# U blocks split in two turns, retrieval head by head, head innermost, and closer gather rows: one transformer layer with a product-key expert layer

## The chip, the cores and the metric

The kernel runs on 1 core of a Trainium2 chip. The metric is the device time of one launch in microseconds; the median of three runs counts. Engines: PE (matmuls), DVE (vector), ACT (scalar, activations), POOL (here the indirect DMAs), SP (the DMA queue for loads and stores).

## What is computed

One layer over 512 tokens of width 1024 in f32: three mixers side by side (stick-breaking attention, a gated recurrence, attention into 256 memory tokens), an output projection, and an expert layer whose experts are single neurons. The last one fills most of the time. Cut to its core:

```
h = rms_norm(x + mixed @ w_out)
q = (h @ w_query).reshape(t, 8 heads, 2, 128)
scores = einsum('thcd,hcnd->thcn', q, sub_keys)          # 128 keys per half
top_s, top_i = top_k(scores, 16)                         # per head and half
cand_s = top_s[..0, :, None] + top_s[..1, None, :]       # 16 x 16 sums
cand_i = top_i[..0, :, None] * 128 + top_i[..1, None, :]
best_s, pos = top_k(cand_s, 16)
gate = softmax(best_s);  expert_idx = take(cand_i, pos)
act = gelu(einsum('td,thkd->thk', h, expert_u[expert_idx]))
out = x + einsum('thk,thkd->td', gate * act, expert_v[expert_idx])
```

There are 128 x 128 = 16384 experts, so `expert_u` and `expert_v` have 16384 rows of 1024 each.

## The kernel before

The work is written as some twenty Python generators ("threads") that a class `Threads` runs by a planner, `Pace`: it keeps a clock for each engine, prices every operation from two cost tables, and lets the thread that is due next record its operations up to its next `yield`. What is recorded is the order of each engine's queue; engines then run in that order and wait for each other by semaphores. A `yield "name"` waits for a flag that another thread sets by `th.set("name")`; a `yield` of a number puts the thread off by that many planned nanoseconds. All engine calls go through one helper (line 203), so the rows below name tiles.

A matmul in f32 quality is made of three (`mm3`): a factor is split into a rounded part (`hi`, written by ACT) and the rest (`lo`, by DVE), and hi·hi, lo·hi and hi·lo are summed. `whi`/`wlo` are those parts of weights, `h2hi`/`h2lo` of the normed tokens, `xhi`/`xlo` of expert rows.

The 512 tokens are four tiles of 128. Up to some 350 us the mixers run. From there the expert layer begins, first for tile 0 (`GT`), then for tiles 1 to 3 (`DENSE`): `outproj` (PE, `op`; DVE adds it into `xr`), `norm2` (ACT `sq`, DVE's short `rv`, `rq`, `rs`, PE transposes `xt`, DVE `mxT`, ACT and DVE `h2hi` and `h2lo`), `query` (PE `qp` or `qf` for q, `qs` for the scores, which ACT copies to `sc` or `sct`), and `topk` on DVE. `query` goes by heads, with a `w` of each head split into `whi` and `wlo`; its matmuls fill up with other work, for GT with the mixers' last transposes.

`topk` takes one tile after another. For each pair of a head's two halves `top16` does MAX, FIND and REPLACE on both, and after a `yield` MAX and FIND again; 8 such units per tile, then 4 on 50 candidates each. Then comes a chain over 128 x 2048 f16 elements (`ge`, `gw`, with the helper tile `tkb`), in which one-hot comparisons and products and `fold` give both key numbers of each pick; `IJ` holds these and the gate. For GT `eidx` holds the row numbers of its experts.

GT's experts are then gathered: `gather` fetches one row per token by an indirect DMA on POOL, four ahead, and DVE multiplies and sums it (`row`, 128 times from `expert_u`, then `xg`, 128 times from `expert_v`). `pace_rows` spaces rows by `GAPS`: 1900 ns until the dense query is done, then 8000 ns until all gates are ready, and from there by the blocks that are left.

The other three tiles go through all 16384 experts: 128 U blocks of 128 experts (`dense`: a block is loaded as `ex` by SP, split into `xhi` and `xlo` in pages of a pool of eight, multiplied in 24 matmuls into `ua`, and ACT writes the gelu `gel`, which is stored), and 128 V blocks (`gel` times gates `G` gives `w`, its parts `whi` and `wlo`, summed in `pin`). Between them stand the gates: `gprep` transposes `IJ` (PE `gt`) and makes `gpg`, `gbuild` one-hots on DVE (`oh`), `grest` finishes them on ACT, `gsum` multiplies them on PE (`gb`), ACT copies to `stg` and stores to `gd` in HBM, from where `G` is loaded. This runs beside the U blocks; when the last gate's flag is set, `dense` puts up to `TRANS` = 9 more U blocks in its order and goes over to V. The flags of the query that `topk` waits for are `q{t}`, one for each tile, set when all heads are done.

Of the kernel before, what the change touches and what calls it, by code (L numbers as in the profile page):

```python
# [8 lines left out]
F32R = mybir.dt.float32r  # L9
# [11 lines left out]
P = 128  # L21
D = 1024
# [18 lines left out]
UA = 3  # L41


GAPS = (1900.0, 8000.0)
BLOCK = 4150.0, 0.95
GP = 8000.0
ND2 = 500.0
# [216 lines left out]
def tile_trunk_layer(ctx: ExitStack, tc: tile.TileContext, x, mem, w_in, w_kv, w_out, w_query,  # L264
# [748 lines left out]
    def query(ts):  # L1013
        yield f"h2{ts[0]}"
        if not kst:
            kst["k"] = [page([P, 8, NKEY], name="keys") for _ in range(2)]
            for i in range(2):
                SP.dma_start(kst["k"][i], keys_t[:, 8 * i:8 * i + 8])
        keys = kst["k"]
        for t in ts:  # L1020
            if t in DENSE[1:]:
                b3 = big3([P, 3, 1024], name="sct")
                sc[t] = [b3[:, i].rearrange("p (g n) -> p g n", g=8) for i in range(2)]
                tka[t] = b3[:, 2]
            else:
                sc[t] = [page([P, 8, P], name="sc") for _ in range(2)]
        pend = []

        def tail():
            t, h, q = pend.pop(0)  # L1030
            b = bank("qx")
            for c in range(2):
                PE.transpose(b[:, c * P:(c + 1) * P], q[:, c * P:(c + 1) * P], ident)
            qT = t2([P, 256], name="qT")
            A.activation(qT, b[:, :256], AF.Copy)
            pend2.append((t, h, qT))

        def tail2():
            t, h, qT = pend2.pop(0)
            b = bank("qs")  # L1040
            for c in range(2):
                PE.matmul(b[:, c * P:(c + 1) * P], qT[:, c * P:(c + 1) * P], keys[h // 4][:, 2 * (h % 4) + c], start=True, stop=True)
            A.activation(sc[t][h // 4][:, 2 * (h % 4):2 * (h % 4) + 2], b[:, :256].rearrange("p (c n) -> p c n", c=2),
                         AF.Copy)

        def tailf():
            qT = [pendf.pop(0), pendf.pop(0)]
            h = donef.pop(0)
            bs = [bank("qs") for _ in range(2)]
            o = [bs[i // 2][:, (i % 2) * 256:(i % 2) * 256 + 256] for i in range(ND)]  # L1050
            for i in range(ND):
                for c in range(2):
                    PE.matmul(o[i][:, c * P:(c + 1) * P], qT[c][:, i * P:(i + 1) * P], keys[h // 4][:, 2 * (h % 4) + c],
                              start=True, stop=True)
            for i, t in enumerate(ts):
                A.activation(sc[t][h // 4][:, 2 * (h % 4):2 * (h % 4) + 2], o[i].rearrange("p (c n) -> p c n", c=2), AF.Copy)

        pend2, pendf, donef = [], [], list(range(QF, PH))
        for h in range(PH):
            W = ws.get()  # L1060
            if h == PH - 1 and ts is DENSE:
                th.set("q_last")
            if ts is DENSE and h >= QF:
                for c in range(2):
                    b = bank("qf")
                    for k in range(KD):
                        w, lw = [x[k // 4][:, k % 4, c * P:(c + 1) * P] for x in W]
                        mm3(b[:, :TD], w, lw, hsl(h2hi, k, 0, TD), hsl(h2lo, k, 0, TD), k == 0, k == KD - 1)
                    qT = t2([P, TD], name="qT")
                    A.activation(qT, b[:, :TD], AF.Copy)  # L1070
                    if pend2:
                        tail2()
                    if pend:
                        tail()
                    elif len(pendf) > 1:
                        tailf()
                    pendf.append(qT)
                    yield
                continue
            for t in ts:  # L1080
                if th.later(f"h2{t}"):
                    yield f"h2{t}"
                b = bank("qp")
                if t == GT:
                    proj_t(W, 0, b[:, :256], *[[h] for h in gat["hT"]])
                else:
                    proj_t(W, DENSE.index(t), b[:, :256], h2hi, h2lo)
                q = t2([P, 256], name="q")
                A.activation(q, b[:, :256], AF.Copy)
                if pend2:  # L1090
                    tail2()
                if pend:
                    tail()
                pend.append((t, h, q))
                yield
        if ts is DENSE:
            th.set("q_mm")
        while pend or pend2 or pendf:
            if pendf:
                tailf()  # L1100
            if pend2:
                tail2()
            if pend:
                tail()
            yield
        for t in ts:
            th.set(f"q{t}")
# [1 line left out]
    tk = {}  # L1109

    def topk(t):
        yield f"q{t}"
        c_start, c_len, c_rank = [c[:, :, None, :].to_broadcast([P, 16, 32, 4]) for c in tkc]
        pa = tka[t] if t in tka else page([P, 1024], name="tka")
        pb = page([P, 1024], name="tkb")
# [2 lines left out]
        def top16(srcs, vs, ix):  # L1118

            for k in (0, 8):  # L1120
                for s, v in zip(srcs, vs):
                    V.max(v[:, k:k + 8], s)
                for s, v, i in zip(srcs, vs, ix):
                    V.max_index(i[:, k:k + 8], v[:, k:k + 8], s)
                if k == 0:
                    for s, v in zip(srcs, vs):
                        V.match_replace(s, v[:, 0:8], s, FILL)
                yield "v"

        for g in range(0, 16, 2):  # L1130
            gs_ = (g, g + 1)
            yield from top16([sc[t][i // 8][:, i % 8] for i in gs_], [vals[:, i] for i in gs_], [idx[:, i] for i in gs_])
        idf = pa[:, 512:768].rearrange("p (h c k) -> p h c k", c=2, k=16)
        V.tensor_copy(idf.rearrange("p h c k -> p (h c) k"), idx)
# [24 lines left out]
            yield from top16([cand[:, i] for i in hs_], [best[:, i] for i in hs_], [pos[:, i] for i in hs_])  # L1159

        IJ = sb.tile([P, 3, 128], F32, name=f"IJ{t}", tag="ij", bufs=2)
        gate = IJ[:, 2].rearrange("p (h k) -> p h k", h=8)
        V.tensor_tensor(gate, best, best[:, :, 0:1].to_broadcast([P, 8, 16]), op=OP.subtract)
        A.activation(gate, gate, AF.Exp)

        posb = pb[:, 400:464].bitcast(F16)
        V.tensor_copy(posb, pos.rearrange("p h k -> p (h k)"))
        ge = page([P, 16, 128], F16, name="ge")
        g4 = ge.rearrange("p r (a b) -> p r a b", b=4)
        V.tensor_tensor(g4, posb.rearrange("p (a b) -> p a b", b=4)[:, None].to_broadcast([P, 16, 32, 4]), c_start,  # L1170
# [3 lines left out]
        def fold(w, dst):  # L1174
# [11 lines left out]
        i1 = pb[:, 528:592].bitcast(F16).rearrange("p (r h) -> p r h", h=8)  # L1186
        V.tensor_copy(i1, idf[:, :, 1, :].rearrange("p h r -> p r h"))
        w = page([P, 16, 128], F16, name="gw")
        V.tensor_tensor(w.rearrange("p r (h k) -> p r h k", h=8), ge.rearrange("p r (h k) -> p r h k", h=8),
                        dI[:, :, :, None].to_broadcast([P, 16, 8, 16]), op=OP.mult)  # L1190
        yield "v"
        yield from fold(w, IJ[:, 0])
        yield "v"
# [6 lines left out]
        V.tensor_tensor(g4, bb.rearrange("p (a b) -> p a b", b=4)[:, None].to_broadcast([P, 16, 32, 4]), c_rank,  # L1200
                        op=OP.is_equal)
        yield "v"
        V.tensor_tensor(ge.rearrange("p r (h k) -> p r h k", h=8), ge.rearrange("p r (h k) -> p r h k", h=8),
                        i1[:, :, :, None].to_broadcast([P, 16, 8, 16]), op=OP.mult)
        yield "v"
        yield from fold(ge, IJ[:, 1])
        yield "v"
# [108 lines left out]
    def dense():  # L1316
# [6 lines left out]
                store[b] = raw([P, D], name="ex")  # L1323
                SP.dma_start(store[b], src[b])

        def split(rw, dst, b, eng, pg):
            if b >= NBLK or b in dst:
                return
            hi = pg([P, D], F32R, name="xhi")
            A.activation(hi, rw[b], AF.Copy)  # L1330
            lo = pg([P, D], F32R, name="xlo")
            eng.tensor_tensor(lo, rw[b], f(hi), op=OP.subtract)
            dst[b] = (hi, lo)

        def u_prep(b):
            for i in range(b, b + 3):
                load(ur, u_t, i)
            split(ur, us, b, V, wpage)

        def u_mm(b):  # L1340
            blocks[0] -= 1
# [86 lines left out]
        pace.late = True  # L1428
        u_prep(0)
        u_prep(1)  # L1430
        yield "q_mm"
        while vi < NBLK:
            ready = all(f"G{t}" in th.flags for t in DENSE)
            if ui < NBLK and (not ready or ui < vi + LA):
                u_prep(ui + 2)
                u_mm(ui)
                ui += 1
                yield "pe"
# [7 lines left out]
            if not pins:  # L1446
                for i in range(3, 3 + UA):
                    load(ur, u_t, ui + i)
                g_load(0)
                while uo and uo[0][0] < 4:  # L1450
                    u_gelu()
                gel_back(0)
                for i in range(min(TRANS, NBLK - ui)):
                    u_prep(ui + 2)
                    u_mm(ui)
                    ui += 1
                    if i == VT:
                        gel_back(1)
                        vhi(0)
                    yield "pe"  # L1460
                gel_back(1)
                vhi(0)
                prep1(0)
                prep2(0)
                prep1(1)
                vhi(1)
                for _ in range(2 * ND):
                    pins.append(bank("pin"))
# [138 lines left out]
```

## Time and profile before

| | |
|---|---|
| median of 3 runs | 1612.44 us (1610.82 to 1612.53) |
| profiled execution | 1616.55 us, of which the span of the instructions is 1614.5 us |
| mean granted clock of PE | 0.988 of full |
| PE busy | 1567.7 us, 97% of the span |
| DVE, ACT, POOL busy | 78%, 49%, 21% |
| chain that ended last | PE 95%, DVE 2%, ACT 1%, DMA 1% |
| DMA | 424 MB, 263 GB/s on average |

An engine's busy share tells little by itself: the stages have different limits. The chain is followed back from the last instruction, at each step to what released it. In timelines, the bracket behind a row is the time that the engine stood idle before it and the instruction that ended this.

### The profile page before, as it was taken

Reading aid. Unit: us, or ns where it says so; the run is one execution under the profiler, and the core shown is the slowest. Engines: PE = TensorE matmul, PEld = TensorE weight load, DVE = VectorE, ACT = ScalarE, POOL = GpSimd, SP = SyncE. Lnnn points to the kernel's source line nnn. Section 1 sums busy time; section 2 is a strip of 40 time slices with the busy share of each in tenths; the row PEclk is TensorE's granted clock in tenths of the full one; section 3 lists DMA queues with packets and bytes.
Section 4 is the critical chain, followed back from the end, with each engine's and each line's share of the span. In section 5 each row is a group of like instructions: output and inputs, shape, how many; then the busy total and the mean of one; then the engine's idle time right before and its main releaser. Section 6 shows DMA issues by size and latency. Waiting matters only on the chain.

```text
span 1614.5 us, 25732 instructions
## 1 busy us (share of the span) xinstructions
PE 1567.7 (97%) x9359; PEld 1436.4 (89%) x9359; DVE 1260.6 (78%) x2499; ACT 790.6 (49%) x1559; POOL 337.8 (21%) x340
## 2 busy tenths in 40 slices
PE   6999999998999999999999999969999999999998
PEld 5998998898999999999999999968888888888886
DVE  5466568779768798778887966739888988998997
ACT  5422258764434336677566777733333333333332
POOL 3000000000251111112011111233343434343430
PEclk9999999999999999999999999979999999999999
DMA  6232102264497767888788889899999999999993
GB/s 248 81 103 79 53 27 91 81 229 163 155 358 251 233 217 246 268 259 282 256 277 264 267 282 292 277 313 407 408 408 399 393 393 380 395 387 396 380 384 121
DMA packets 164239, 424.03 MB, mean 263 GB/s; under 512 B 13584, under 2 KB 62736, under 8 KB 164112
## 3 DMA queue, kind: packets, MB, share of 16 engines
q1 hardware_dynamic: 68256, 238.21, 41.0%
q0 software_dynamic: 36864, 134.23, 22.7%
q10 hardware_dynamic: 58992, 49.95, 9.3%
q8 instruction: 73, 1.20, 0.3%
q14 instruction: 54, 0.44, 0.1%
HBM read 368.20 MB, written 54.13 MB: 262 GB/s over the span
## 4 chain that ended last, share of the span: by engine, by line
PE 95%; DVE 2%; ACT 1%; DMA 1%; issue 0%; DVEq 0%; SPq 0%; ACTq 0%
PE ua L203 33%; PE pin L203 32%; PE pf L203 5%; PE pt L203 4%; PE qf L203 4%; PE sz L203 3%; PE gb L203 3%; PE op L203 3%; PE qp L203 2%; PE hs L203 2%; PE so L203 1%; PE qs L203 1%; DMA gd<-stg 1%; ACT se L203 0%; PE mo L203 0%; PE nt L203 0%
## 5 line engine op out<-in xcount | busy, mean ns | idle before, releaser
L203 DVE TENSOR_TENSOR xlo<-ex,xhi 128x1024 fp32r<-128x1024 f32 x256 | 312.5, 1221 | 118.6 <-ACT xhi L203 109.2
L203 POOL DMA_INDIRECT row<-in_u_rows_dram,eidx x128 | 156.1, 1219 | 977.0 <-ACT whi L203 402.2
L203 PE MATMUL ua<-h2hi,xhi 128*128 128x384 f32 x1024 | 348.6, 340 | 0.0
L203 PE MATMUL ua<-h2hi,xlo 128*128 128x384 f32 x1024 | 342.8, 335 | 0.0
L203 PE MATMUL ua<-h2lo,xhi 128*128 128x384 f32 x1024 | 342.5, 335 | 0.0
L203 ACT ACTIVATE whi<-w 128x384 fp32r<-128x384 f32 (+1 forms) x205 | 144.9, 724 | 345.1 <-DVE w L203 325.8
L203 PE MATMUL pin<-xhi,whi 128*128 128x512 f32 x768 | 300.1, 391 | 12.1 <-ACT whi L203 12.1
L203 PE MATMUL pin<-xlo,whi 128*128 128x512 f32 x768 | 299.9, 391 | 0.9 <-DVE xlo L203 0.9
L203 PE MATMUL pin<-xhi,wlo 128*128 128x512 f32 x768 | 299.7, 390 | 0.0
L203 ACT ACTIVATE xhi<-ex 128x1024 fp32r<-128x1024 f32 x256 | 268.3, 1049 | 28.6 <-DMA ex<-in_v_rows_dram 14.2
L203 DVE TENSOR_TENSOR wlo<-w,whi 128x384 fp32r<-128x384 f32 (+1 forms) x204 | 161.0, 804 | 99.7 <-ACT whi L203 51.2
L203 POOL DMA_INDIRECT row<-in_v_rows_dram,eidx x128 | 164.7, 1286 | 251.2 <-DVE xg L203 175.8
L203 PEld LDWEIGHTS ua<-h2lo,xhi 128*128 128x128 f32 x1024 | 192.5, 188 | 0.0
L203 PEld LDWEIGHTS ua<-h2hi,xhi 128*128 128x128 f32 x1024 | 192.2, 188 | 0.0
L203 PEld LDWEIGHTS ua<-h2hi,xlo 128*128 128x128 f32 x1024 | 192.2, 188 | 0.0
L203 PEld LDWEIGHTS pin<-xhi,whi 128*128 128x128 f32 x768 | 144.8, 189 | 42.5 <-ACT whi L203 12.4
L203 PEld LDWEIGHTS pin<-xlo,whi 128*128 128x128 f32 x768 | 144.8, 189 | 31.5 <-DVE xlo L203 1.4
L203 PEld LDWEIGHTS pin<-xhi,wlo 128*128 128x128 f32 x768 | 144.7, 188 | 30.3
L203 DVE SCALAR_TENSOR_TENSOR xg<-row,wgt,xg 128x1024 f32<-128x1024 f32 x128 | 163.9, 1280 | 1.0
L203 DVE CUSTOM_DVE_ANT_0 row<-row,xr 128x1024 f32<-128x1024 f32 x128 | 154.6, 1218 | 6.8 <-issue 6.6
L203 ACT ACTIVATE oh<-oh,gpg 128x128 f16<-128x128 f16 x384 | 126.5, 436 | 26.7 <-DVE oh L203 6.8
L203 ACT ACTIVATE gel<-ua 128x384 f32<-128x384 f32 x128 | 62.7, 490 | 156.4 <-PE ua L203 151.0
(255 smaller groups left out, 2299.5 us busy)
## 6 DMA issues: line engine op xcount, KB each, us to landing
ex<-in_u_t_dram SPq DMA_DIRECT2D x128, 512.0 KB
ex<-in_v_rows_dram SPq DMA_DIRECT2D x128, 512.0 KB
gd<-stg ACTq DMA_DIRECT2D x48, 512.0 KB
G<-gd SPq DMA_DIRECT2D x48, 512.0 KB
gel<-gel ACTq DMA_DIRECT2D x63, 384.0 KB
gel<-gel SPq DMA_DIRECT2D x63, 384.0 KB
w<-in_w_query_dram SPq DMA_DIRECT2D x32, 512.0 KB
w<-in_w_in_dram SPq DMA_DIRECT2D x26, 512.0 KB
```

The source lines that it names most:

```text
L203: r = fn(*args, **kw)
```

## The change

Four things. (1) The U blocks: `u_prep` now loads and rounds a block (`xhi`, on ACT) three blocks ahead of its matmuls, and a new `u_rest` takes the rest (`xlo`, on DVE) two blocks ahead, where both stood at two blocks; loads are made as far ahead as before. (2) `query` sets a flag `s{t}_{h}` behind each head's score copy, and `topk` waits for the flag of each unit's head in place of `q{t}`. (3) The gate, the positions and the two products hold the 128 picks of a token as [k, h], the head innermost, where they stood as [h, k]; so the factor that is the same for all k of a head is no longer repeated along the innermost axis. (4) `GAPS` for the rows after the query falls from 8000 to 6000 ns.

```diff
-GAPS = (1900.0, 8000.0)
+GAPS = (1900.0, 6000.0)
...
             A.activation(sc[t][h // 4][:, 2 * (h % 4):2 * (h % 4) + 2], b[:, :256].rearrange("p (c n) -> p c n", c=2),
                          AF.Copy)
+            th.set(f"s{t}_{h}")
...
                 A.activation(sc[t][h // 4][:, 2 * (h % 4):2 * (h % 4) + 2], o[i].rearrange("p (c n) -> p c n", c=2), AF.Copy)
+                th.set(f"s{t}_{h}")
...
     def topk(t):
-        yield f"q{t}"
+        yield f"s{t}_0"
...
             gs_ = (g, g + 1)
+            yield f"s{t}_{g // 2}"
...
-        gate = IJ[:, 2].rearrange("p (h k) -> p h k", h=8)
+        gate = IJ[:, 2].rearrange("p (k h) -> p h k", h=8)
...
-        V.tensor_copy(posb, pos.rearrange("p h k -> p (h k)"))
+        V.tensor_copy(posb.rearrange("p (k h) -> p h k", h=8), pos)
...
-        V.tensor_tensor(w.rearrange("p r (h k) -> p r h k", h=8), ge.rearrange("p r (h k) -> p r h k", h=8),
-                        dI[:, :, :, None].to_broadcast([P, 16, 8, 16]), op=OP.mult)
+        V.tensor_tensor(w.rearrange("p r (k h) -> p r k h", h=8), ge.rearrange("p r (k h) -> p r k h", h=8),
+                        dI[:, :, None, :].to_broadcast([P, 16, 16, 8]), op=OP.mult)
...
-        V.tensor_tensor(ge.rearrange("p r (h k) -> p r h k", h=8), ge.rearrange("p r (h k) -> p r h k", h=8),
-                        i1[:, :, :, None].to_broadcast([P, 16, 8, 16]), op=OP.mult)
+        V.tensor_tensor(ge.rearrange("p r (k h) -> p r k h", h=8), ge.rearrange("p r (k h) -> p r k h", h=8),
+                        i1[:, :, None, :].to_broadcast([P, 16, 16, 8]), op=OP.mult)
...
         def u_prep(b):
-            for i in range(b, b + 3):
+            for i in range(b, b + 2):
                 load(ur, u_t, i)
-            split(ur, us, b, V, wpage)
+            if b < NBLK:
+                us[b] = [wpage([P, D], F32R, name="xhi")]
+                A.activation(us[b][0], ur[b], AF.Copy)
+
+        def u_rest(b):
+            if b < NBLK:
+                lo = wpage([P, D], F32R, name="xlo")
+                V.tensor_tensor(lo, ur[b], f(us[b][0]), op=OP.subtract)
+                us[b].append(lo)
...
             if ui < NBLK and (not ready or ui < vi + LA):
-                u_prep(ui + 2)
+                u_prep(ui + 3)
+                u_rest(ui + 2)
                 u_mm(ui)
```

How the rows of an engine's queue stand at three places, first DVE in the query of GT, from the mixers' sum `oss` on. The `wlo` are parts of query weights, one pair for each head. Before:

```order
L203 TENSOR_REDUCE oss_3466<-o_3415 128x12
L203 TENSOR_SCALAR rv_3469<-oss_3466 128x12
L203 TENSOR_TENSOR wlo_3473<-w_3321,whi_3471 128x1024
L203 TENSOR_TENSOR wlo_3477<-w_3323,whi_3475 128x1024
L203 TENSOR_TENSOR rq_3522<-rr_3519 128x12
```

The same place after:

```order
L203 TENSOR_REDUCE oss_3474<-o_3423 128x12
L203 TENSOR_SCALAR rv_3477<-oss_3474 128x12
L203 MAX tka_3415<-sc_3205 128x8 x2
L203 MAX_INDEX tka_3415<-tka_3415,sc_3205 128x8 x2
L203 TENSOR_TENSOR wlo_3485<-w_3321,whi_3483 128x1024
L203 TENSOR_TENSOR wlo_3489<-w_3323,whi_3487 128x1024
L203 MAX tka_3415<-sc_3205 128x8 x2
L203 MAX_INDEX tka_3415<-tka_3415,sc_3205 128x8 x2
L203 MATCH_REPLACE sc_3205<-tka_3415,sc_3205 128x128 x2
L203 TENSOR_TENSOR rq_3540<-rr_3531 128x12
```

A second half of a top-k unit (MAX and MAX_INDEX, which the profile calls MAX8 and FIND_INDEX8) now stands ahead of this pair, and a first half behind it; seven rows further on, in both orders, the `wlo` of head 7 follow.

DVE again, where the first rows of the gather arrive, during head 3 and 4 of the dense query; `eidx` holds the row numbers, `row` with `act` is one gathered row (an ISA pair). Before:

```order
L203 SCALAR_TENSOR_TENSOR eidx_4565<-IJ_4342 128x128
L203 TENSOR_TENSOR wlo_4569<-w_4236,whi_4567 128x1024
L203 TENSOR_TENSOR wlo_4573<-w_4238,whi_4571 128x1024
L203 ISA row_4619,act_4617<-row_4619,xr_2623 128x1024
L203 ISA act_4617 128x1
```

The same place after, from the first row on:

```order
L203 ISA row_4550,act_4548<-row_4550,xr_2623 128x1024
L203 ISA act_4548 128x1
L203 MAX tka_4540<-sc_4268 128x8 x2
L203 MAX_INDEX tka_4540<-tka_4540,sc_4268 128x8 x2
L203 ISA row_4552,act_4548<-row_4552,xr_2623 128x1024
L203 ISA act_4548 128x1
L203 MAX tka_4540<-sc_4268 128x8 x2
L203 MAX_INDEX tka_4540<-tka_4540,sc_4268 128x8 x2
L203 MATCH_REPLACE sc_4268<-tka_4540,sc_4268 128x128 x2
L203 ISA row_4554,act_4548<-row_4554,xr_2623 128x1024
L203 ISA act_4548 128x1
L203 TENSOR_TENSOR wlo_4606<-w_4280,whi_4604 128x1024
```

Before, the pair of `wlo` behind `eidx` is head 4's; after, head 3's stands there, and head 4's (here `wlo_4606`) has moved behind the first three rows.

Last, DVE in the U blocks where the third dense tile's one-hots begin (`gpg` is made from the transposed `IJ`, `oh` are the one-hots). Before:

```order
L203 TENSOR_SCALAR gpg_10372<-gt_10285 128x128
L203 CAST gpg_10372<-gt_10285 128x2x64x2
L203 CAST gpg_10372<-gpg_10372 128x128
L203 TENSOR_TENSOR gpg_10372<-gpg_10372 128x128
L203 ISA row_10007,act_4617<-row_10007,xr_2623 128x1024
L203 ISA act_4617 128x1
L203 TENSOR_TENSOR oh_10380<-io2_6103,gpg_10372 128x1024
L203 TENSOR_TENSOR oh_10380<-oh_10380,gpg_10372 128x512
L203 TENSOR_TENSOR oh_10383<-io2_6103,gpg_10372 128x1024
```

The same place after:

```order
L203 TENSOR_SCALAR gpg_10428<-gt_10354 128x128
L203 CAST gpg_10428<-gt_10354 128x2x64x2
L203 CAST gpg_10428<-gpg_10428 128x128
L203 TENSOR_TENSOR gpg_10428<-gpg_10428 128x128
L203 TENSOR_TENSOR oh_10433<-io2_5831,gpg_10428 128x1024
L203 TENSOR_TENSOR oh_10433<-oh_10433,gpg_10428 128x512
L203 TENSOR_TENSOR oh_10436<-io2_5831,gpg_10428 128x1024
L203 TENSOR_TENSOR oh_10436<-oh_10436,gpg_10428 128x512
L203 TENSOR_TENSOR oh_10452<-io2_5831,gpg_10428 128x1024
```

The row of the gather that stood between `gpg` and the first one-hot is gone from there. On PE, between this tile's `gt` and its second to fourth `gb` stand three U blocks, where four stood.

## Rows read from the trace of the kernel before

**Rows 1.** PE's waits, whole run: waited for, us in total, times, longest us

```profile
PE pin L203 <- ACT whi L203: 12.1, 1, 12.1
...
PE qf L203 <- issue: 2.5, 3, 1.2
```

**Rows 2.** Busy us (x instructions) by stretch: PE, PEld, DVE, ACT, POOL; clock, DMA, GB/s

```profile
700.00:800.00 100.00, 100.00 (x664) 97.76 (x663) 86.99 (x211) 66.30 (x153) 14.87 (x13) 1.00 0.83 274
...
1200.00:1300.00 100.00, 100.00 (x443) 82.80 (x442) 89.59 (x105) 35.77 (x50) 38.36 (x30) 1.00 1.01 398
```

**Rows 3.** Timeline of DVE in GT's query: start, us, operation [idle before]

```profile
340.38 2.36 DVE L203 TENSOR_TENSOR wlo<-w,whi 128x1024 fp32r<-128x1024 f32 x2 [1.89 <-ACT whi L203]
...
360.28 0.48 DVE L203 MAX8 tka<-sc 128x8 f32<-128x128 f32 x2
...
361.71 0.68 DVE L203 TENSOR_TENSOR mxl<-mxT,mxh 128x512 fp32r<-128x512 f32 x1
362.31 0.48 DVE L203 MAX8 tka<-sc 128x8 f32<-128x128 f32 x2
...
363.23 0.47 DVE L203 MAX8 tka<-sc 128x8 f32<-128x128 f32 x2
```

**Rows 4.** Timeline of PE, single rows from 349 to 941 us

```profile
349.70 0.39 PE L203 MATMUL qp<-wlo,h2g 128*128 128x256 f32 x1 [0.27 <-DVE wlo L203]
...
399.74 1.97 PE L203 MATMUL xt<-ident,sq 128*128 128x128 f32 x8 [3.68 <-ACT sq L203]
...
441.09 0.33 PE L203 MATMUL qf<-h2hi,wlo 128*128 128x384 f32 x1
441.26 0.33 PE L203 MATMUL qf<-h2hi,whi 128*128 128x384 f32 x1
...
449.51 0.34 PE L203 MATMUL qf<-h2hi,wlo 128*128 128x384 f32 x1 [1.20 <-issue]
...
940.66 0.49 PE L203 MATMUL gt<-ident,IJ 128*128 128x128 f32 x3
```

**Rows 5.** Timeline of DVE at the first rows of the gather

```profile
431.79 0.28 DVE L203 SCALAR_TENSOR_TENSOR eidx<-IJ 128x128 int32<-128x128 f32 x1
...
441.82 1.23 DVE L203 CUSTOM_DVE_ANT_0 row<-row,xr 128x1024 f32<-128x1024 f32 x1 [6.64 <-issue]
```

**Rows 6.** DVE's groups by shape, 391 to 960 us: busy us, mean ns

```profile
L203 DVE TENSOR_TENSOR gw<-ge,tkb 128x2048 f16<-128x2048 f16 x4 | 9.1, 2284 | 0.0
...
L203 DVE TENSOR_TENSOR ge<-ge,c 128x2048 f16<-128x2048 f16 x4 | 4.9, 1219 | 0.0
```

**Rows 7.** Timeline of DVE and ACT at the third dense tile's first one-hots

```profile
944.63 1.23 DVE L203 TENSOR_TENSOR xlo<-ex,xhi 128x1024 fp32r<-128x1024 f32 x1 [3.53 <-ACT xhi L203]
...
947.91 0.69 DVE L203 TENSOR_TENSOR oh<-io,gpg 128x1024 f16<-128x1024 f16 x1
...
948.63 1.32 ACT L203 ACTIVATE oh<-oh,gpg 128x128 f16<-128x128 f16 x4 [2.29 <-DVE oh L203]
948.98 0.69 DVE L203 TENSOR_TENSOR oh<-io,gpg 128x1024 f16<-128x1024 f16 x1
```

**Rows 8.** Timeline of ACT, SP and DVE from the last U to the first V block

```profile
1062.59 1.33 ACTq L203 DMA_DIRECT2D gd<-stg  x2
...
1072.77 0.32 SPq L203 DMA_DIRECT2D G<-gd  x1
...
1077.70 0.56 DVE L203 TENSOR_TENSOR w<-gel,G 128x384 f32<-128x384 f32 x1 [17.58 <-issue]
...
1080.58 1.06 ACT L203 ACTIVATE xhi<-ex 128x1024 fp32r<-128x1024 f32 x1 [14.21 <-DMA ex<-in_v_rows_dram]
```

**Rows 9.** Stretches around the first V block, columns as in rows 2

```profile
1067.00:1072.00 5.00, 3.00 (x18) 2.68 (x16) 0.00 (x0) 0.00 (x0) 0.94 (x1) 1.00 1.06 358
...
1082.00:1089.00 7.00, 5.96 (x13) 4.40 (x14) 5.94 (x9) 2.99 (x5) 1.05 (x2) 0.50 1.03 416
```

**Rows 10.** Timeline of DVE at the end

```profile
1609.26 1.28 DVE L203 SCALAR_TENSOR_TENSOR xg<-row,wgt,xg 128x1024 f32<-128x1024 f32 x1
```

More of the change, by code (lines that the diff above doesn't have):

```diff
@@ L1324, in load @@
                 SP.dma_start(store[b], src[b])
[L1326 to L1333, printed above, removed]
         def u_prep(b):
-            for i in range(b, b + 3):
+            for i in range(b, b + 2):
                 load(ur, u_t, i)
-            split(ur, us, b, V, wpage)
+            if b < NBLK:
[6 more added lines that the diff above has]
+                us[b].append(lo)
         def u_mm(b):
@@ L1430, in dense @@
         u_prep(1)
+        u_rest(0)
+        u_prep(2)
+        u_rest(1)
         yield "q_mm"
@@ L1453, in dense @@
                 for i in range(min(TRANS, NBLK - ui)):
-                    u_prep(ui + 2)
+                    u_prep(ui + 3)
+                    u_rest(ui + 2)
                     u_mm(ui)
```

## The prediction

> **What bounds the kernel now.** I read the share of busy time first, then PE's waits, then the table of stretches, and only then timelines at the places where PE waits. The table [rows 2] shows a PE that is busy for 100 of 100 us in the middle of the U blocks and again in the V blocks, at the full granted clock, while DVE is at 87 to 90. In those stretches nothing that DVE, ACT or a queue gains can shorten the run, unless it removes a wait somewhere else. What can move is the list of PE's waits [rows 1]: 12.1 us before the first V block and 2.5 of `issue` in the query; then 3.68 before the last of three `xt` transposes and 0.27 for a `wlo` [rows 4], and the waits of the first 300 us, which the change does not touch. A price per microsecond follows: where PE is the bound, a microsecond of wait is a microsecond of the run. A longer wait costs more, since after one the clock is at half for a while: from 1082 to 1089 us PE works at a granted clock of 0.50 of full, that is at 1.2 of 2.4 GHz [rows 9], right after it stood idle for some 12 us; 7 us at half speed lose 3.5 us.
>
> **The head-innermost layout.** It changes no count. Per token tile `gw` (2284 ns, x4) and the second product on `ge`, which is of the same form, have a factor repeated along the innermost axis; after the change that axis holds 8 neighbouring heads. The nearest row is an operation of the same 2048 elements and the same type without such a repeat, `ge<-ge,c` at 1219 ns [rows 6]. I take that one: 8 x (2284 - 1219) = 8.5 us of DVE. The dearer end is no gain at all; the conversion of `posb` and the subtraction for `gate` now write with a stride, on 128 elements each, which I take as nothing, covered by PE at 100 of 100 us. All four tiles' products lie beside PE's matmuls, so by itself this is worth 0; it counts through DVE's queue below.
>
> **Top-k by head, GT's query.** A top-k unit now waits for one head's scores and not for all eight, so units enter DVE's queue among the `wlo` of the same query. A unit's first half (two MAX, two FIND, two REPLACE) takes 361.71 - 360.28 = 1.43 us, its second 363.23 - 362.31 = 0.92 us [rows 3]. The first half lands ahead of the `wlo` at 340.38, which today follows 1.89 us of idle: covered, cost 0. The next second half (0.92) and first half (1.43) land ahead of the `wlo` of head 7, with no idle time to hide them. Today PE already waits 0.27 us for that `wlo` at 349.70 [rows 4], so there is no slack: 0.92 + 1.43 = 2.35, less a little that the earlier `wlo` gains: **+2.2 us** (0.5 if DVE's small operations there shrink, 3.9 if the wait halves the clock for 3.5 us).
>
> **Norm of the dense tiles.** PE waits 3.68 us at 399.74 and less at two more `xt` [rows 4]; each waits for ACT's `sq`, which waits for four short DVE operations that stand behind top-k pieces. These units are earlier now, so at this point DVE is already in the 50-wide folds of the candidates, and two tiles' short operations stand back to back. Adding up DVE's rows between the same marks in both orders, the first tile comes later and the last about 0.9 us earlier: **-0.9 us** (-2 to +1).
>
> **First rows of the gather.** `eidx` is done at 431.79 and the first row reaches DVE at 441.82, 10.0 us later, of which DVE stood idle 6.64 [rows 5]. Today head 4's `wlo` stands ahead of that wait; now it stands behind it and behind three rows. What is queued behind the waiting row operation is thus a `wlo` that PE wants: PE reads the first `wlo` of head 4 at 441.09 [rows 4], about 442.4 with the +2.2 and -0.9 above. DVE has some 5 us less to do before `eidx` (2.1 from GT's two products, some 3 of units that slipped into idle time), so I put `eidx` at 426 and the first row at 436.0. Then three rows (1.3 us each with the read of the sum), two second halves or so of units between them (0.92 and 1.43), and one `wlo` of 1.2: 436.0 + 3.9 + 2.35 + 1.2 = 443.4 against 442.4. **+1.0 us** (0 if `eidx` is at 425, +4 if at 429).
>
> **The `issue` wait.** At 449.51 PE waits 1.20 us for nothing that the profile shows [rows 4], the first of three such waits of 2.5 us together [rows 1], with a lower clock after them; in all about 3.4 us. It falls into the stretch in which the first ten rows are fetched. The change leaves ten rows there, a few us earlier: **0** (-3.4 if it vanishes, +2 if it lasts longer). The Trainium skill (Runtime: NRT & Kernel Launch, Instruction fetch mechanics) says that instructions are refilled by DMA in blocks of 256 and that this is hidden by the pace of issue. By that these waits could not be a fetch; the trace has an idle PE with no semaphore behind it while the DMA engines are full, which speaks against the word hidden, and no run here shows yet which it is. By the rule the wait would follow some other cause, and the term stays 0 either way.
>
> **U two and three blocks ahead.** ACT's `xhi` moves one block earlier, DVE's `xlo` stays. Today DVE waits for `xhi`, 3.53 us of it at 944.63 [rows 7], and PE does not wait for DVE there: 100 of 100 us [rows 2]. The hi and lo pages alternate over eight buffers, so now `xlo` reuses the page of the block three before, and DVE may wait for PE's end of that block in place of `xhi`. A block is 24 matmuls 0.17 us apart [rows 4], some 4.15 us, and `xlo` has over one block of slack left: **0**. One place is tight: for the third dense tile the order puts its second to fourth `gb` behind three U blocks after `gt` where four stood. Today DVE needs 3.3 us from 944.63 to the first `oh` (`xlo`, four small operations, a row of 1.14) and 1.07 for each pair of `oh` [rows 7]. After, that is 2.1 without the row, 3.2 for three pairs, 3.4 for another `xlo`, a row and the fourth pair, and 1.3 on ACT: 10.0 us, to 954.6 if DVE starts as late as today. The last of these `gb` is due at 940.66 + 0.6 for `gt` and a `gb` [rows 4] + 3 x 4.15 = 953.7. **+1.0 us** (0 to 3).
>
> **Rows every 6 us and not 8.** By the order 109 rows stand ahead of the last one-hot instead of 89, some 20 x 1.3 = 26 us of DVE moved from the V stage to the U stage. DVE has the room there (87 of 100 us [rows 2]), and in the V stage PE is the bound, so both are 0. DMA share in the U stage rises from 0.83 [rows 2] by about a tenth: no wait.
>
> **From U to V.** In both orders the last `gb` stands behind the same U block, and two more blocks follow. The chain that PE waits for: the store of the last gates issued at 1062.59, its reload at 1072.77, `w` at 1077.70, `xhi` at 1080.58 (its load was queued behind the reload), `whi`, `pin` [rows 8]. The longest link is the store: 10.2 us, at a DMA share of 1.06 and 358 GB/s in its second half [rows 9], in which gathered rows of 0.5 MB each (1.5 us of all engines at that rate) are ahead of it. In the new order of POOL the rows stand some 3 us earlier against the last `gb`, so one to two rows less are ahead: **-2 us** (-5.6 if the store takes the 4.9 us that the reload takes up to `w`, and +2 if a row comes right behind it). PE does not get more U blocks to cover it.
>
> **The end.** Today a last `xg` row at 1609.26 follows the last sums on DVE [rows 10], and only then is `xg` stored; in the new order no row stands there. The store issues about 0.8 us earlier: **-0.8 us** (-1.3 to 0).
>
> **Sum.** +2.2 - 0.9 + 1.0 + 0 + 0 + 1.0 + 0 - 2.0 - 0.8 = +0.5 us. The profiled execution took 1616.55 us, so it would take 1617.0; the median of the runs shown, 1612.44, lies 4.1 us below it with the same waits, so my forecast is 1613.0.
>
> **Rivals.** *Faster: the store to `gd` is freed.* If the rows come early enough, the store takes 5 us and not 10, PE's idle time falls to about 6.5 us, and about half of the half-clock stretch goes with it: -5.6 - 1.7 in place of -2, that is 1607.5. For it: the store is the one long link, and the engines are full because of rows. Against it: in the new order rows are also more frequent, and some still stand next to the store. *Slower: head 4's `wlo` behind the row wait.* If DVE's earlier pieces bring `eidx` nothing but the products' 2.1 us, `eidx` is at 429.7, the `wlo` at 447.1, and PE waits 4.7 us; with about 1.7 for the clock that is +5.4 in place of +1.0: 1617.4. It decides from `eidx` at 428 on. For it: DVE is full from 391 on, and the 6.64 us of idle have no cover but this `wlo`. Against it: seven units move forward by the order. *The change doesn't do what it says*: the first gate work stands eight U blocks earlier, yet the last `gb` stands behind the same block, so the earlier start is not an earlier end. I hold this for likely; it is part of the forecast.
>
> **How the numbers follow.** One measurement of this kernel can tell about 0.2%, 3.2 us, from no change. Forecast (within 3.2 us of 1612.4): 0.44. The freed store, or the `issue` wait gone with it: 0.29, mostly 1604 to 1609. The late `wlo`, or a larger loss at head 7 through the clock: 0.27, mostly 1616 to 1621. The likeliest case alone spans 1609 to 1616. To hold 8 in 10, the range takes -7.5 (store freed) and +7.5 (the late `wlo` with the upper end at head 7): 1605 to 1620.
>
> **What would show it.** In the profile after: `qp<-DVE wlo` of about 2.5 us near 350; the last `xt` wait near 3; DVE's first row near 436 and a `qf` wait of about 1 for `wlo`; `gw` and the last `ge` near 1.22 us; PE at 100 in the U and V stages; 10 us and not 12 ahead of the first `pin`. The forecast is wrong if PE shows a wait for `xlo` or `gb` in the U stage over 3 us, if the gap ahead of `pin` falls below 7, or if top-k pieces hold up more than one `wlo`.

## The result, and the profile after

The changed kernel is slower: median 1623.09 us (1615.82 to 1630.80, 6 runs) against 1612.74 (1610.82 to 1615.89) for the kernel before, a ratio of 1.0061 [1.0034, 1.0087]. Timed again on two later occasions it was at 1.0031 [1.0014, 1.0048] on the first, and at 1.0052 [1.0033, 1.0071], 1.0037 [1.0023, 1.0050] and 1.0039 [1.0017, 1.0061] on the second: 0.3 to 0.6% slower, 5 to 10 us. The forecast was 1613.0 in 1605 to 1620. The six executions of the changed kernel spread over 15 us, those of the kernel before over 5; on the later occasions it was 7 against 12 and 14 against 7, so the changed kernel is not always the wider one. Three more executions of it, of 1970 to 2625 us at a mean granted clock of 0.555 to 0.745, are left out of the ratios and spreads.

Its first profiled execution happens to be the fastest of the six, 1615.82 us with a span of 1614.1. PE's waits over the whole run (waited for, us in total, times, longest):

```profile
PE pin L203 <- ACT whi L203: 9.5, 1, 9.5
PE xt L203 <- ACT sq L203: 5.2, 3, 3.4
...
PE qp L203 <- DVE h2lo L203: 2.8, 1, 2.8
PE qp L203 <- DVE wlo L203: 1.5, 2, 1.1
```

Against [rows 1, 4]: the wait before the first V block is 2.6 us shorter, the `issue` wait is gone, the waits for `xt` are 1.7 us less, and a wait that was not there, 2.8 us for `h2lo`, and a longer one for `wlo` have come. The places, from PE's timeline:

```profile
353.34 0.39 PE L203 MATMUL qp<-wlo,h2g 128*128 128x256 f32 x1 [1.10 <-DVE wlo L203]
...
412.77 0.58 PE L203 MATMUL qp<-whi,h2lo 128*128 128x256 f32 x1 [2.78 <-DVE h2lo L203]
```

DVE ahead of the second of these:

```profile
404.64 1.23 DVE L203 TENSOR_TENSOR ge<-tkb,c 128x2048 f16<-128x2048 f16 x1
...
408.23 1.21 DVE L203 TENSOR_TENSOR gw<-ge,tkb 128x2048 f16<-128x2048 f16 x1
409.37 0.75 DVE L203 TENSOR_TENSOR h2lo<-mxT,h2hi 128x256 fp32r<-128x256 f32 x2
410.04 2.35 DVE L203 TENSOR_TENSOR wlo<-w,whi 128x1024 fp32r<-128x1024 f32 x2
412.31 0.74 DVE L203 TENSOR_TENSOR h2lo<-mxT,h2hi 128x256 fp32r<-128x256 f32 x2
```

Tile 0's top-k is early enough now that its 128x2048 operations stand among the `h2lo` of the dense tiles. Each of the three tiles has two pairs of these; the fifth of the six starts at 412.31, and PE, which is through with everything else, starts on it at 412.77. Before, the first of those 128x2048 operations came behind the sixth pair:

```profile
409.54 0.74 DVE L203 TENSOR_TENSOR h2lo<-mxT,h2hi 128x256 fp32r<-128x256 f32 x2
...
412.29 1.23 DVE L203 TENSOR_TENSOR ge<-tkb,c 128x2048 f16<-128x2048 f16 x1
```

The layout does what it says (DVE's groups by shape, 391 to 960 us: busy us, mean ns):

```profile
L203 DVE TENSOR_TENSOR ge<-ge,tkb 128x2048 f16<-128x2048 f16 x4 | 4.9, 1220 | 0.0
L203 DVE TENSOR_TENSOR gw<-ge,tkb 128x2048 f16<-128x2048 f16 x4 | 4.9, 1213 | 0.0
```

`gw` took 2284 ns [rows 6] and takes 1213. The Trainium skill (VectorE: DVE Perf Modes, Mode 2×_1P) asks for 16-bit elements one step apart for two results a cycle, and the two rows agree: only the repeat along the innermost axis went.

### The profile page after: what moved, and what is told of

The parts are those of the page before. It is cut to its first block, busy times and chain, and to the rows that moved or that the text cites. A ratio compares the mean times of both kernels' runs of the same rounds, so it can differ in the third digit from the quotient of the medians.

```text
span 1614.1 us, 25742 instructions
## 1 busy us (share of the span) xinstructions
PE 1569.7 (97%) x9359; PEld 1438.1 (89%) x9359; DVE 1256.5 (78%) x2499; ACT 792.8 (49%) x1559; POOL 330.2 (20%) x340
## 4 chain that ended last, share of the span: by engine, by line
PE 94%; DVE 3%; ACT 1%; DMA 1%; issue 0%; SPq 0%; ACTq 0%; DVEq 0%
PE ua L203 33%; PE pin L203 32%; PE pf L203 5%; PE pt L203 4%; PE qf L203 4%; PE op L203 3%; PE gb L203 3%; PE sz L203 3%; PE hs L203 2%; PE qp L203 1%; PE so L203 1%; PE qs L203 1%; ACT se L203 1%; PE nt L203 0%; PE mo L203 0%; DVE wlo L203 0%
## 5 line engine op out<-in xcount | busy, mean ns | idle before, releaser
L203 ACT ACTIVATE xhi<-ex 128x1024 fp32r<-128x1024 f32 x256 | 268.4, 1050 | 23.4 <-DMA ex<-in_v_rows_dram 11.6
L203 POOL DMA_INDIRECT row<-in_v_rows_dram,eidx x128 | 156.7, 1224 | 314.8 <-DVE xg L203 199.3
L203 ACT ACTIVATE oh<-oh,gpg 128x128 f16<-128x128 f16 x384 | 126.6, 436 | 29.4 <-DVE oh L203 10.2
```

Of the source, the lines that this page charges most:

```text
L203: r = fn(*args, **kw)
```

## The experiments

All times are medians, all ratios are to the kernel before on the same occasion. A ratio is not the quotient of two medians, and the kernel before itself had medians of 1612.7 to 1616.2 us on these occasions, so times of different paragraphs are compared by their ratios.

**Each edit undone.** The changed kernel again, and with one edit taken back in each: GAPS; the split of the U blocks; the flags of top-k.

```diff
# undo_gaps
-GAPS = (1900.0, 6000.0)
+GAPS = (1900.0, 8000.0)
# undo_split
...
-                u_prep(ui + 3)
-                u_rest(ui + 2)
+                u_prep(ui + 2)
...
# undo_heads
-        yield f"s{t}_0"
+        yield f"q{t}"
...
-            yield f"s{t}_{g // 2}"
```

> The changed kernel once more, to see its spread: six executions lay between 1615.8 and 1630.8 us, where those of before lay between 1610.8 and 1615.9. If the loss is a fixed wait, all executions agree within some 5 us and lie near 1621. If it is a wait that comes and goes (a transfer that is late in some executions), they spread over 10 us or more again, and the profile of this one shows waits of PE, and stretches at half clock, that the first profile (1615.8 us) does not have.

> The changed kernel with GAPS back at 8000: 20 rows fewer in the U stage. Theory R (closer rows fill the DMA engines in the U stage and make loads late in some executions): back to 1611 to 1615 us, small spread. Theory S (the split U blocks) and theory H (top-k by head): no change, 1618 to 1625 us with the spread of the changed kernel.

> The changed kernel with both parts of a U block two blocks ahead, as before. Theory S (DVE's xlo now waits for PE's end of the block three before, and the load has one block less to land ahead of ACT's xhi, so an execution with a late load stops ACT, DVE and PE): back to 1611 to 1615 us, small spread. Theories R and H: no change, 1618 to 1625 us.

> The changed kernel with top-k waiting for all heads, as before. Theory H (top-k pieces ahead of h2lo and wlo on DVE: 2.8 us of wait at qp<-h2lo and half clock behind it, some 4 us in the first profile): 4 us faster than the changed kernel, and the spread gone if the lost time comes from there. Theories R and S: no change, 1618 to 1625 us.

Measured: 1621.2 (1.0031), 1631.07 (1.0098 [1.0073, 1.0124]), 1618.86 (1.0029 [1.0013, 1.0045]), 1634.62 (1.0125 [1.0097, 1.0153]). The second profile of the changed kernel (1619.71 us) has the waits of the first and no new one. All three theories missed: no single edit taken back takes the loss away, and without GAPS or without the flags the kernel is much slower than with both. PE's waits tell why. Without the flags:

```profile
PE pin L203 <- ACT whi L203: 16.0, 1, 16.0
...
PE gb L203 <- ACT oh L203: 9.4, 7, 3.1
```

and its stretches at the transition (columns as in rows 2):

```profile
1085.00:1106.00 21.00, 4.02 (x9) 2.84 (x10) 4.56 (x7) 3.67 (x7) 3.57 (x4) 0.50 1.00 371
```

The gates come so late that all U blocks are done before the last `gb`; PE waits for gates, then 16 us for the first V block, and its clock stays at half from 1072 to 1106 us. Without GAPS it is the other way round:

```profile
PE pin L203 <- ACT xhi L203: 8.4, 5, 3.6
PE pin L203 <- DVE xlo L203: 6.1, 8, 1.2
```

Twelve U blocks stand behind the last `gb`. That is more than the nine that the transition may hold; the rest are drawn out between V blocks to the end (the last `ua` ends at 1610.6 us), and V blocks wait for their own parts in places all over the V stage. So GAPS and the flags are two hands on one scale: where the last `gb` stands against the end of the U blocks.

**Both off, and two cures for the query.**

```diff
# undo_heads_gaps: undo_heads and undo_gaps together; split and layout are left
# norm_first, in topk ahead of IJ
+        if t == GT:
+            yield f"h2{DENSE[-1]}"
# gt_whole
-        yield f"s{t}_0"
+        yield f"q{t}" if t == GT else f"s{t}_0"
```

> The kernel before once more, for a second profile. Theory I (the 2.5 us of issue wait at 449 us and the slow stretch behind it come only in some executions, and the profiled one had them, so the median is some 4 us shorter): a profile of about 1613 us without that wait. Rival (the wait is a fixed part of every execution): it stands there again, at the same matmul. Ratio 1.000 in both.

> The changed kernel, but top-k of tile 0 goes on to its 128x2048 operations only when the norm of the last dense tile is through. Theory H2 (the loss is the 2.8 us of qp<-h2lo near 410 us, where h2lo stands behind those operations on DVE, and the half clock behind it): that wait gone, 4 to 5 us faster than the changed kernel, 1615 to 1617. Theory C (the loss is only in how long the clock stays at half after the gap from U to V): no change against the changed kernel, 1621.

> The changed kernel, but tile 0's top-k waits for all eight heads as before; the dense tiles' top-k still goes head by head. Theory H1+H2 (the loss is in the query and norm up to 412 us: 2.1 us at head 7's wlo, 2.8 at h2lo, and the clock): the query of tile 0 as in the kernel before, 5 to 7 us faster than the changed kernel, 1614 to 1616, with the transition still as short as the changed kernel's. Theory C: no change, 1621. Rival (tile 0's top-k is then late, eidx late, and the first rows hold up head 4's wlo): a wait of qf for wlo near 445 us of 3 us or more, so only 1 to 3 us faster.

> The changed kernel with both the flags of top-k and GAPS as before, so only the split of the U blocks and the layout are left. With the flags alone undone it took 1634, with GAPS alone undone 1631. Theory B (the two edits balance each other: closer rows take the DVE time that earlier top-k gives, and with only one of them the last gate comes too late or too early for the nine U blocks that cover it): 1611 to 1616, like the kernel before. Rival (each of the two would be needed by the split or the layout): 1625 or more.

Measured: 1617.01 (1.0005 [0.9987, 1.0024]), 1615.85 (0.9998 [0.9972, 1.0025]), 1617.42 (1.0004 [0.9983, 1.0025]), 1608.85 (0.9950 [0.9934, 0.9966]); the kernel before was at 1616.18 on this occasion. The second profile of the kernel before has 0.2 us of `issue` wait where the first had 2.5 [rows 1]:

```profile
PE qf L203 <- issue: 0.2, 1, 0.2
```

so that wait belongs to some executions and not to the kernel: of the twenty profiles of this document, only the first has it in that size. But theory I also put the time at some 1613 us without it, and this execution took 1617.73; that the wait is what set the first profile 4 us above the median is not shown. The ratios of both cures lie where the change had cost something, though their intervals still touch that of the changed kernel. The traces say it more sharply: norm_first has no wait for `h2lo` left, gt_whole none for `h2lo` and only the 0.3 of before for `wlo`. The first U block starts at 484.0 and 481.1 us with them, at 485.7 and 485.6 in the two profiles of before, at 488.5 and 490.8 in two of the changed kernel. Over all twenty profiles, the ten in which PE waits for `h2lo` start it at 485.9 to 490.8 us, the ten others at 481.1 to 485.7, on average 4.4 us earlier. What the cures do not remove is the spread: the twelve executions of norm_first lie between 1611.9 and 1630.8 us. And split with layout alone is a gain: its wait before the first V block is down to half.

```profile
PE pin L203 <- ACT whi L203: 6.0, 1, 6.0
```

**Which of the two gains, and where the last gb should stand.** Split alone and layout alone on the kernel before; GAPS 6500 in the changed kernel; GAPS 9000 with split and layout.

> The kernel before with only the split of the U blocks (xhi three ahead, xlo two). With split and layout together it was 0.5% faster than before, and the last gb then stood behind the third block from the end on, with four U blocks left to cover the store and reload of the gates. Theory A (that gain is the split's: by the order it alone moves the last gb forward by two U blocks): the same 0.5% faster, some 8 us, gap before the first pin near 6 us. Rival L (the gain is the layout's 8.5 us of DVE): no change against before, gap 12.

> The kernel before with only the head-innermost layout; the order of every queue stays as it was, 8.5 us of DVE are saved in the gate stage. Theory A: no change against before (within 0.2%), since the last gb stands behind the same U block and PE is the bound. Rival L: 0.5% faster.

> The changed kernel with GAPS 6500 in place of 6000: by the order the last gb stands three U blocks earlier, with five blocks behind it to cover store and reload of the gates, and no more than the nine that the transition may hold. Theory B (where the last gb stands against the end of the U blocks decides the gap): the gap of 9.5 to 10.8 us before the first pin falls below 2, some of the half clock behind it goes too: 10 to 15 us faster than the changed kernel, 0.3 to 0.6% faster than before. Rival (the gap is set by the store's own slowness among the rows, so the chain only starts earlier and stretches): 3 us or less faster than the changed kernel.

> Split and layout with top-k's flags as before, and GAPS 9000 in place of 8000: by the order the last gb stands three U blocks earlier than with 8000, seven blocks cover the gates. Theory B: the gap of 6.0 us goes to 0 and half clock with it, 6 to 10 us faster than with 8000, about 1% faster than before. Rival (rows moved to the V stage make DVE the bound there, as with GAPS alone undone, which took 1631): slower than with 8000.

Measured: 1607.37 (0.9965 [0.9951, 0.9979]), 1612.81 (0.9997 [0.9986, 1.0008]), 1610.71 (0.9983 [0.9966, 0.9999]), **1600.20 (0.9915 [0.9899, 0.9932])**. The gain is the split's; the layout's 8.5 us of DVE are worth nothing by themselves, as forecast. The place of the last `gb` in the order, counted in U blocks behind it, sorts the waits before the first `pin` of all kernels but one:

| kernel | U blocks behind the last gb | wait before the first pin, us | ratio |
|---|---|---|---|
| undo_heads | 0 | 16.0 | 1.0125 |
| undo_split | 1 | 10.6 | 1.0029 |
| before | 2 | 12.1 and 13.1 | 1 |
| layout_only | 2 | 11.3 | 0.9997 |
| changed | 2 | 9.5 to 11.6 | 1.003 to 1.006 |
| split_only | 4 | 6.0 | 0.9965 |
| undo_heads_gaps | 4 | 6.0 | 0.9950 |
| gaps_6500 | 5 | 2.9 | 0.9983 |
| split_layout_gaps_9000 | 7 | 0 | 0.9915 |
| undo_gaps | 12 | 1.9, and 14.5 more in V blocks | 1.0098 |

The exception is undo_split, with one block and a shorter wait than before. The time from the last `gb` to the first `pin` is not fixed: 15.0 us in undo_split, 18.1 to 21.7 in the changed kernel and before, 22.9 to 24.0 with four and five blocks. So the chain stretches when it has more cover, and GAPS 6500, with three blocks or some 12 us more of cover, takes only 7 to 9 us off the changed kernel's wait; its theory B had the place right, and put what is left of the wait below 2 us where it is 2.9. The ratios follow only in part, since gaps_6500 keeps the loss in the query. In the changed kernel the split moves the last `gb` by one block only, and taking it out there (undo_split) makes no difference that can be told.

In the last but one, PE's waits of the transition are down to 0.2 us, and the clock stays full there; the stretches of 1035 to 1082 us:

```profile
1035.00:1070.00 35.00, 35.00 (x212) 34.54 (x211) 21.02 (x31) 13.51 (x27) 15.36 (x13) 1.00 0.98 366
1070.00:1082.00 12.00, 12.00 (x55) 9.93 (x54) 12.00 (x20) 4.77 (x7) 7.40 (x6) 1.00 1.03 407
```

The rival (fewer rows in the U stage make DVE the bound in V) did not show: fewer rows there cost nothing as long as no U block is left over.

**Both cures together, and the spread.**

> The changed kernel with both cures: tile 0's top-k goes on to its 128x2048 operations only when the norm of the last dense tile is through, and GAPS 6500. If the two losses are separate (5 us in the query, 8 to 10 at the gap): they add up, 1604 to 1607 us, 0.4 to 0.6% faster than before. Rival (one gain eats the other, since DVE's work only moves): 1609 to 1612, like GAPS 6500 alone.

> The changed kernel, one more look. Theory C (slow executions differ by how long the clock stays at half behind a wait that every execution has, above all behind the gap from U to V): the same waits as in the first two profiles, and if it is over 1621 us, longer stretches at half clock, by about half a microsecond of time for each microsecond of it. Rival W (a wait that only slow executions have, such as a late load in the U stage): a new wait of PE of 2 us or more.

> The changed kernel, one more look, as after_look1: theory C longer stretches at half clock with the same waits, rival W a new wait of PE of 2 us or more.

> The changed kernel, one more look, as after_look1: theory C longer stretches at half clock with the same waits, rival W a new wait of PE of 2 us or more.

Measured: norm_first_6500 1606.61 (0.9946 [0.9929, 0.9963]): the two losses are separate and add up; against GAPS 6500 alone (0.9983) the cure of the query is worth 0.37%, and the two intervals do not touch. Two of three further profiles of the changed kernel are of executions of 1624.74 and 1625.37 us, and both have a wait that the profiles at 1615.8, 1618.6 and 1619.7 do not have. The timelines of ACT, DVE and PE in the longer of the two, 1034 to 1045 us:

```profile
1034.08 1.21 ACT L203 ACTIVATE stg<-gb 128x256 f32<-128x256 f32 x4 [2.31 <-DMA gd<-stg]
1035.14 1.33 ACT L203 ACTIVATE oh<-oh,gpg 128x128 f16<-128x128 f16 x4
1036.32 1.07 ACT L203 ACTIVATE xhi<-ex 128x1024 fp32r<-128x1024 f32 x1
...
1037.41 1.22 DVE L203 TENSOR_TENSOR xlo<-ex,xhi 128x1024 fp32r<-128x1024 f32 x1 [5.33 <-ACT xhi L203]
...
1044.80 1.15 PE L203 MATMUL gb<-oh 128*128 128x128 f16 x7 [3.27 <-ACT oh L203]
```

ACT stands 2.31 us at a `stg` until a store of gates has read its page; `oh` and `xhi` stand behind it on ACT, DVE waits 5.33 us for that `xhi`, and PE in the end 3.27 us for an `oh`, with half clock after. The last `gb` ends at 1071.8 us in that execution, at 1064.7 in the first: 7 us. So rival W (a new wait) holds for those executions and theory C (the clock alone) does not. What is late are stores of gates: one issued near 1024 us lands after 10.4 to 13.5 us in these two, after 7.0 to 8.6 in the three profiles without the wait. It is no mark of the changed kernel alone: in the profiles of norm_first (two waits, 2.6 us) and gt_whole (3.7 us), between 1023 and 1040 us, a `gb` waits for `oh` too.

**Are the pages the cause?** One page more, with one load buffer less to make room, and the load buffer alone.

```diff
-NPG, NRAW, NW4, NT2 = 16, 7, 8, 8
+NPG, NRAW, NW4, NT2 = 17, 6, 8, 8
```

> The changed kernel with 17 pages in place of 16 and, for the room, 6 load buffers in place of 7; the last gb stands where it stood. Theory P (pages come round too soon, so stg on ACT and oh on DVE wait for the stores that still read them, and in slow executions the wait reaches PE at gb): the waits of stg and oh for gd and gel fall from 9 to 17 us to below 5, no gb wait, and the spread shrinks to 1616 to 1620. Rival T (the stores are late by the traffic, whatever the pages): the same waits and 1621 again.

> The changed kernel with 6 load buffers in place of 7 alone, the control for the run with 17 pages. Loads are made at most five blocks deep in the U stage, so the sixth is enough: the same as the changed kernel, 1621. If it is slower by 2 us or more, the gain of the 17th page is larger than that run shows.

Measured: 1621.71 (1.0060 [1.0039, 1.0082]) and 1619.54 (1.0037 [1.0024, 1.0050]). With 17 pages the waits of `stg` and `oh` for stores in the profile fall (`stg` for `gd` 4.3 us, `oh` for `gel` 0.9, none of `oh` for `gd`, where the control with 16 pages has 7.4, 4.2 and 3.7), and the time does not. So theory P holds for the waits and not for the time: the spread, 1619 to 1632, is still there. That its profile has no `gb` wait says little, since it is of its fastest execution. What makes the stores late in some executions, and where the longer executions with 17 pages lose their time, stays open.

## Why the prediction was wrong, point by point

- *Layout*: right. 1213 ns against the 1219 taken, and worth 0 alone (layout_only).
- *GT's query*: the mechanism and size held. PE waits 1.10 us at 353.34, and 0.4 each at two more places, where one wait of 0.27 stood; against the kernel before, PE loses 2.1 us between the query's start and head 7. Forecast +2.2. One sign that was to speak against the forecast did come: two `wlo` are held up, at 347.41 and 353.34, and not one.
- *Norm of the dense tiles*: **the step that failed.** The part that was counted is right: the `xt` waits fall by 1.7 us against the first profile before and by 0.9 against the second, forecast -0.9. What was not counted is the next reader in the same norm. I followed the short operations up to the transposes and stopped there; behind them come `h2lo`, which now share DVE with tile 0's 128x2048 operations, and PE waits 2.8 us for the fifth pair of six, with 3.4 us at half clock behind it that the first profile before did not have there. In all ten profiles with that order PE waits 2.4 to 4.1 us for `h2lo`, in none of the ten others. Taking only those operations out of the way (norm_first) removes the wait and brings the ratio from 1.003 to 1.006 down to 1.000 [0.9972, 1.0025]. The term was -0.9 and should have been about +3: -1.7 for `xt`, +2.8, and an estimated +1.7 for 3.4 us at half speed. With it the forecast would have been some 1617, still short of the median; the rest is in part in the U blocks below, in part open.
- *First rows*: no wait of `qf` for `wlo`. `eidx` was at 428.6, later than the 426 taken, but the first row came 5.9 us behind it and not 10.0, at 434.48; the fetch took 4.7 us from its issue on POOL at 429.83, where the one before took 8.8 from 433.01. Why it was so much shorter no run shows. So the slower rival's condition came true, `eidx` behind 428, and its wait did not; that this term cost nothing was luck.
- *The issue wait*: it vanished here, and in the second profile of the kernel before too. The sum started from the median, 4.1 us below the profile, "with the same waits"; that the execution at the median has the same waits was not known, and the second profile, without this one, took 1617.73 us. So what the 4.1 us are stays open. The Trainium skill (Runtime: NRT & Kernel Launch, Instruction fetch mechanics) holds fetch to be hidden; what the wait was, no run here shows.
- *U blocks*: 0 was right for the first profile, and the tight place at 954 us did not wait. The term missed that a wait of this kind (`gb` for ACT's `oh`) comes in some executions only, near 1043 us, and then costs some 7. So this is the second term that was too small: 0 in three of the five profiles of the changed kernel, some 7 us in the other two. A term taken from one execution has no spread in it.
- *U to V*: forecast -2, measured -2.6 and -1.3 in two profiles, and down to -0.5 in the longest. Right in size, and for the reason given: in the first profile the store's link, from its issue to the reload's, is 6.9 us where it was 10.2, and the reload up to `w` takes 1.3 us more.
- *The end*: -0.2 of the forecast -0.8. The store of `xg` does issue earlier, at 1609.57 for 1610.57, but the run still ends 5.7 us behind the end of the last `pin`, where it was 5.9.
- *The rival that the change doesn't do what it says* was half right: heads and GAPS cancel each other at the last `gb`. I did not see that the split alone moves it forward by two blocks, because I compared only the whole change with before; that gain of 0.35% is gone again in the whole change. *The faster rival* had the right place (the gap) and the wrong lever: not the store, which did become shorter, but the number of blocks that cover it. Its 1.7 us for the clock have no support either: with the gap at 6.0 us (split_only, undo_heads_gaps) PE still works 7.5 and 6.6 us at half clock behind the first `pin`, where before it was 7.1. *The slower rival* named a `wlo` on DVE; it was an `h2lo`, 30 us earlier.

The balance by ratios: the split -0.35%; whether the layout with it adds anything (0.9950 against 0.9965) the intervals do not tell; then the flags and GAPS together +0.8 to 1.1%. Of this the query takes some 0.3%, by the 4.4 us at the first U block and by the 0.37% above; the rest goes to the last `gb`, with two U blocks behind it in place of four, and to the `gb` wait of some executions. The last two shares are only measured as a whole.

## What to carry to other kernels

Where a planner sets the order, count from the order itself how much of the covering work stands behind the last producer of a stage; here two, four and seven blocks gave 9.5 to 13, 6 and 0 us of gap, and that count, which needs no run, sorts the gaps of all kernels above but one. When work is let into a queue earlier, follow the stage that it enters to its last reader, and take an edit's parts one by one against the kernel before, since two parts can cancel each other and hide a third that gains. A term read from one execution needs the spread of several: a wait that reaches PE in some of them moves the median too.

## What the runs showed of the hardware

What PE loses to the clock behind the gap from U to V hardly depends on how long the gap is. In the sixteen profiles with gaps of 6.0 to 16.0 us the granted clock falls to 0.50 (1.2 of 2.4 GHz) while PE stands idle there, in undo_heads already before. What costs time is the part of that stretch behind the first `pin`, and it is 4.6 to 7.8 us long: 5.8 behind 9.5 us (the changed kernel), 7.1 behind 12.1 (before), 5.2 behind 16.0 (undo_heads), 7.5 behind 6.0 (split_only). Behind 2.9 us (gaps_6500) it was 3.4, behind 2.5 (norm_first_6500) 6.8, and without a gap (split_layout_gaps_9000) the clock stays full. At half speed that is an estimated 2 to 4 us on top of any of the longer gaps, and shortening one saves its own length and little more until it is nearly gone.

Two profiles of the kernel before have the first `pt`, a matmul of the mixers, 0.7 us apart (63.3 and 64.1 us), five of the changed kernel 1.1, and a half-clock stretch falls now near 255, now near 294 us; so a microsecond or two between two profiles means nothing.
